# Attention: scores and turned queries and keys ahead of the transposed probabilities, within a slot's group of short matmuls

## The chip, the cores and the metric

The kernel runs on one core of one Trainium2 chip. The metric is the device time of one execution in microseconds (us); lower is better. TensorE (PE in the profile, with its weight loads as PEld), VectorE (DVE), ScalarE (ACT), GpSimd (POOL) and the DMA queue of SyncE (SP) each work through a list of their own and wait for each other by semaphores.

## The reference

A decoder trunk of two layers over one sequence of 1024 tokens of width 1024, in float32. The first layer's mixer has two parts that share one input projection: a gated spatial mixing of 128-token chunks, and an attention of eight heads of width 64. Only the attention bears on the change:

```
B_BRANCHES = ((128, 1), (512, 4), (2048, 16))       # window, dilation
qh, kh = rms_norm(heads(q), q_g), rms_norm(heads(k), k_g)
for window, dilation in B_BRANCHES:
    # keys of the own and the previous block of 128, of every dilation-th token
    s = where(valid, q @ k.T * hd ** -0.5, NEG)
    m = max(s); p = exp(s - m); den = sum(p)
    o = (p @ v) / den;  lse = m + log(den)
b_out = sum over branches of softmax(lse) * o
```

After it come the output projection, a gated MLP with a causal convolution, and a second layer with gated linear attention and the same kind of MLP.

## The kernel before

The attention works by pairs of heads, four pairs in all. A pair has 16 units: eight near units (kind "n", dilation 1, one for each block of 128 queries) and eight far units (kind "d", tokens by stride 4, with the third branch folded in by a mask). `order` lists them as near 0 to 7 and far 0 to 7 of pair 0, then of pair 1, and so on: 64 units, each with a slot of its own. I count slots from 0; slots 16 to 23, for instance, are the near units of the second pair.

A unit has three steps on TensorE. `score` multiplies queries by keys (two fp32r matmuls, the high and the low part of the keys, for each of the two heads) into the PSUM tile `sc`. VectorE adds the mask and takes the row minimum of the negated scores (L895), and ScalarE makes the exponentials in `sm` and their sum (L896). `turn` transposes `sm` on TensorE into the PSUM tile `pP` (L916), which is copied to `pT`: by VectorE for even units, by ScalarE for odd ones (L918). `output` multiplies `pT` by the values into `po` (L927). The three steps of one unit stand in three slots that follow each other: the scores in its own, the transposes in the next, the output in the one after.

For near units the queries and keys of a block are first turned themselves: `Pair.turn` transposes the duplicated keys `kd` (L997) and the split queries `qs` (L122) into the PSUM tile `tk`, of which there is one buffer. ScalarE and VectorE split it into `kT` (L116, L117), and ScalarE copies the queries to `qT` (L1002). This is done two slots ahead of the unit, so 30 of the 64 slots hold such turns.

Between these short matmuls TensorE works at the projection of the next pair (`pj`, later `pv` and `pu`, L218): `take(share)` issues 13, 12 or 21 of its matmuls in each slot. Meanwhile ScalarE and VectorE make the next weights `wq`, `wv` from raw ones (L767, L768), normalise queries and keys (L964 to L973), and combine the near and far results of the pair before (`combine`, L1037 to L1056, in the slots of near units 4 and 6).

TensorE's order is the order in which the code issues (`pin` keeps it). The order on the other engines is set by a scheduler that works out when each instruction would be ready, so it can move when TensorE's order is changed. Buffers: `sm` 3, `pT` 2, and in PSUM `sc` 2, `pP` 2, `pj` 2, `po` 1, `tk` 1.

Of the kernel before, what the change touches and what calls it, by code (L numbers as in the profile page):

```python
# [67 lines left out]
def trunk(ctx: ExitStack, tc: tile.TileContext, a, out):  # L68
# [581 lines left out]
    def even(gm_open):  # L650
        with ExitStack() as st:
# [69 lines left out]
            with tc.tile_pool(name="at", bufs=2, reuse_waits="tile") as at, \  # L721
                    tc.tile_pool(name="av", bufs=1, reuse_waits="tile") as av:
                return attention(ps, at, av, pq, pq0, par0, wx, wq0, gqk, masks, rest, gm_open)
# [152 lines left out]
    def attention(ps, at, av, pq, pq0, par0, wx, wq0, gqk, masks, rest, gm_open):  # L876
# [59 lines left out]
        class Pair:  # L936
# [46 lines left out]
            def parts(self, n):  # L983
                qn = self.qn[n]
                qs = pq.tile([P, 2, P], F32R, tag="qs", bufs=2, name=f"qs{self.p}{n}")
                split([qs[:, :, :64], qs[:, :, 64:]], heads(qn[:, :P]), hi=G.tensor_copy)
                kd = pq.tile([P, 2, P], F32, tag="ks", bufs=2, name=f"kd{self.p}{n}")
                G.tensor_tensor(kd.rearrange("p h (x c) -> p h x c", x=2),
                                heads(qn[:, P:])[:, :, None, :].to_broadcast([P, 2, 2, 64]),
                                gqk[:, None, None, :].to_broadcast([P, 2, 2, 64]), op=ALU.mult)  # L990
                self.qs[n] = qs, kd
# [39 lines left out]
        def combine(q, g):  # L1031

            p, os = q.p, [q.near[g]["ot"], q.on[g]]
            nm = [o[:, :, 128:130] for o in os]
            den = [o[:, :, 130:132] for o in os]
            M = small.tile([P, 4, 2], F32, tag="cM", bufs=2, name=f"cM{p}{g}")
            tc.keep_in_program_order(V.tensor_tensor(M, nm[0], nm[1], op=ALU.min))  # L1037
            e = small.tile([P, 2, 4, 2], F32, tag="cE", bufs=2, name=f"cE{p}{g}")
            for i in range(2):
                V.tensor_sub(e[:, i], M, nm[i])  # L1040
            A.activation(e, e, AF.Exp)
            return lambda: combined(p, g, os, den, e)
# [22 lines left out]
        def weights():  # L1065
            if slot and spread:
                spread.pop(0)()
# [4 lines left out]
        def mix(when):  # L1072
            while mixes and when(mixes[0]):
                mixes.pop(0)[2]()
# [16 lines left out]
        def take(m):  # L1091
            for _ in range(m):
                ins = next(stream, None)
                if ins is not None:
                    if pairs[0].done > 1:
                        tc.keep_in_program_order(ins)
# [16 lines left out]
        def turns(i):  # L1113
            p, kind, n = place_of(i)
            if kind == "n":
                pairs[p].turn(n)
# [9 lines left out]
        ended, scored = [], []  # L1126
        for slot, (p, kind, n) in enumerate(order):
            share = RATE[0] if slot < NT else RATE[1] if len(pairs) < PAIRS or pairs[-1].done < NT else RATE[2]
            parts(slot + 3)
            score, turn, output = pairs[p].near_unit(n) if kind == "n" else pairs[p].far_unit(n)  # L1130
            for f in ended:
                f()
            for f, _ in scored:
                f()
            score()
            turns(slot + 2)
            mix(lambda m: m[0] <= slot)
            weights()
            take(share // 2)
            weights()  # L1140
            take(share - share // 2)
            ended, scored = [f for _, f in scored], [(turn, output)]
            if kind == "n" and p and n in (4, 6):
                combine(pairs[p - 1], n // 2 - 2)()
# [588 lines left out]
```

## Time and profile before

| | us |
|---|---|
| median of 3 runs | 2114.88 |
| lowest, highest | 2114.22, 2115.79 |
| the profiled execution's own time | 2114.53 |
| its span, first to last instruction | 2112.8 |
| TensorE busy | 2102.1 |
| VectorE busy | 1533.2 |
| ScalarE busy | 1058.7 |

The attention's slots lie between about 34 and 318 us of the span. In the profile a row of the timeline has the start, the time from there to the end of the last one merged into it, engine, line, operation, the tiles written and read, their shape and the count. Starts of weight loads (PEld) show the pace of TensorE better than the ends of matmuls, which are modelled. A row of the waits has the engine and tile that waited, the releaser, and the total, the count and the longest. Tile names in the trace lack their last numbers: `sm1n` is any `sm` of the near units of pair 1. A wait of TensorE lengthens the run directly; a wait of another engine does only if TensorE has to wait for it in turn.

### The profile page before, as it was taken

Reading aid. Unit: us, or ns where it says so; the run is one execution under the profiler, and the core shown is the slowest. Engines: PE = TensorE matmul, PEld = TensorE weight load, DVE = VectorE, ACT = ScalarE, POOL = GpSimd, SP = SyncE. Lnnn points to the kernel's source line nnn. Section 1 sums busy time; section 2 is a strip of 40 time slices with the busy share of each in tenths; the row PEclk is TensorE's granted clock in tenths of the full one; section 3 lists DMA queues with packets and bytes.
Section 4 is the critical chain, followed back from the end, with each engine's and each line's share of the span. In section 5 each row is a group of like instructions: output and inputs, shape, how many; then the busy total and the mean of one; then the engine's idle time right before and its main releaser. Section 6 shows DMA issues by size and latency. Waiting matters only on the chain. (4 is left out here: it accounts for less than half of the span.)

```text
span 2112.8 us, 29740 instructions
## 1 busy us (share of the span) xinstructions
PE 2102.1 (99%) x10440; PEld 1793.6 (85%) x10440; DVE 1533.2 (73%) x2486; ACT 1058.7 (50%) x2063; POOL 471.3 (22%) x479
## 2 busy tenths in 40 slices
PE   8999999999999999999999999999999999999999
PEld 8999988888888888888899888888888888888887
DVE  7566564678889888655578777886788788785554
ACT  7566564455444444444454466745544444444443
POOL 5344310014335243000010011101334243220000
PEclk9999999999999999999999999999999999999999
DMA  7122314854544444765654243596544454458564
GB/s 256 53 75 65 106 46 173 306 197 145 177 142 159 160 163 168 259 220 205 216 182 158 88 137 125 182 325 240 193 163 151 167 164 158 152 181 294 208 227 162
DMA packets 170278, 367.08 MB, mean 174 GB/s; under 512 B 17632, under 2 KB 61408, under 8 KB 170128
## 3 DMA queue, kind: packets, MB, share of 16 engines
q1 hardware_dynamic: 169984, 365.05, 50.5%
q8 instruction: 82, 1.34, 0.3%
q14 instruction: 68, 0.56, 0.1%
q10 hardware_dynamic: 144, 0.13, 0.0%
HBM read 248.39 MB, written 115.93 MB: 172 GB/s over the span
## 5 line engine op out<-in xcount | busy, mean ns | idle before, releaser
L117 DVE TENSOR_TENSOR da<-ar,da 128x512 fp32r<-128x512 f32 x154 | 106.2, 690 | 154.7 <-ACT da L116 154.5
L116 ACT CAST da<-ar 128x512 fp32r<-128x512 f32 x154 | 96.0, 623 | 212.7 <-PE pdQ L427 99.5
L218 PE MATMUL po<-wo,hq 128*128 128x512 f32 x768 | 183.0, 394 | 0.0
L218 PEld LDWEIGHTS po<-wo,hq 128*128 128x128 f32 x768 | 142.0, 188 | 28.5 <-DVE hq L117 0.3
L218 PE MATMUL pv<-wv,hq 128*128 128x512 f32 (+2 forms) x768 | 139.7, 339 | 0.0
L427 PE MATMUL pdC<-dw,da 128*128 128x512 f32 x528 | 134.8, 390 | 0.0
L427 PE MATMUL pdB<-dw,da 128*128 128x512 f32 x528 | 134.8, 390 | 0.0
L218 PEld LDWEIGHTS pv<-wv,hq 128*128 128x128 f32 x768 | 119.4, 189 | 14.7
L218 PE MATMUL pj<-wq,hq 128*128 128x384 f32 x672 | 128.6, 339 | 0.0
L427 PEld LDWEIGHTS pdC<-dw,da 128*128 128x128 f32 x528 | 99.0, 188 | 20.5
L427 PEld LDWEIGHTS pdB<-dw,da 128*128 128x128 f32 x528 | 98.8, 188 | 20.3
L218 PEld LDWEIGHTS pj<-wq,hq 128*128 128x128 f32 x672 | 114.8, 188 | 0.0
L286 POOL TENSOR_TENSOR S1g<-rg 128x512 f32<-128x512 f32 x20 | 28.5, 1427 | 378.6 <-DMA wsd<-D 262.2
L117 DVE TENSOR_TENSOR dw<-wr,dw 128x512 fp32r<-128x512 f32 x154 | 105.7, 686 | 8.4 <-ACT dw L116 8.0
L161 POOL TENSOR_SCALAR rn<-ssq 128x1 f32<-128x1 f32 x22 | 8.8, 402 | 424.9 <-ACT h L181 242.4
L427 PE MATMUL pdO<-dw,da 128*128 128x512 f32 x396 | 100.5, 389 | 0.0
L116 ACT CAST dw<-wr 128x512 fp32r<-128x512 f32 x154 | 95.0, 617 | 8.6 <-DMA wr<-in_w_dn 4.9
L427 PEld LDWEIGHTS pdO<-dw,da 128*128 128x128 f32 x396 | 74.3, 188 | 15.4
L351 DVE SCALAR_TENSOR_TENSOR t<-g,cw,t 128x1022 f32<-128x1022 f32 x44 | 74.8, 1700 | 0.1
L335 DVE TENSOR_TENSOR g<-g,s1g 128x512 f32<-128x512 f32 x22 | 16.4, 745 | 77.8 <-ACT s1g L334 77.8
L350 DVE SCALAR_TENSOR_TENSOR t<-g,cw,t 128x1023 f32<-128x1023 f32 x44 | 57.3, 1302 | 14.8 <-ACT t L349 14.8
L161 POOL TENSOR_SCALAR ro<-oss 128x1 f32<-128x1 f32 x32 | 9.4, 292 | 255.6 <-ACT og L1448 255.6
(1052 smaller groups left out, 5440.6 us busy)
## 6 DMA issues: line engine op xcount, KB each, us to landing
ar<-actd SPq DMA_DIRECT2D x70, 512.0 KB, 3.6
rd<-in_w_down SPq DMA_DIRECT2D x44, 512.0 KB, 3.6
wsd<-D SPq DMA_DIRECT2D x88, 256.0 KB, 2.3
rg<-in_w_gate SPq DMA_DIRECT2D x40, 512.0 KB, 3.6
ru<-in_w_up SPq DMA_DIRECT2D x40, 512.0 KB, 4.5
wr<-wsd SPq DMA_DIRECT2D x40, 512.0 KB, 4.3
actd<-t SPq DMA_DIRECT2D x66, 256.0 KB, 2.2
wr<-in_w_dn SPq DMA_DIRECT2D x30, 512.0 KB, 5.0
```

The lines of the kernel that those rows point to most:

```text
L116: (hi or A.copy)(dst[0], src)
L117: (lo or V.tensor_sub)(dst[1], src, f32(dst[0]))
L161: eng.tensor_scalar(r, ssq, 1.0 / n, EPS, op0=ALU.mult, op1=ALU.add)
L218: yield T.matmul(o, L[i], R[jj][:, sl], start=(k == 0 and (ii, jj) == PASSES[0]), stop=(k == nk - 1 and (ii, jj) == PASSES[-1]))
L286: G.tensor_tensor(sums[name], x, y, op=op)
L335: V.tensor_add(C22, C22, s1)
L350: V.scalar_tensor_tensor(t[:, 1:], g[:, : S - 1], w(1), t[:, 1:], op0=ALU.mult, op1=ALU.add)
L351: V.scalar_tensor_tensor(t[:, 2:], g[:, : S - 2], w(0), t[:, 2:], op0=ALU.mult, op1=ALU.add)
L427: T.matmul(o, L[ii][:, t * P : t * P + P], R[jj], skip_group_check=more, start=start and not more and (ii, jj) == PASSES[0], stop=stop and ...
```

## The change

In each slot the two lines that run `turn` of the unit before (`scored`) move behind the scores, the turned queries and keys, and the mixing. The outputs (`ended`) stay ahead.

```diff
             for f in ended:
                 f()
-            for f, _ in scored:
-                f()
             score()
             turns(slot + 2)
             mix(lambda m: m[0] <= slot)
+            for f, _ in scored:
+                f()
             weights()
             take(share // 2)
```

TensorE in slot 21 (near unit 5 of pair 1), before; `pP1n4` are the transposed probabilities of unit 4, `sc1n5` the scores of unit 5, `tk17` the turned keys and queries of block 7:

```order
L916 MATMUL pP1n4_1871<-ident_78,sm1n40_1819 128x128 x2
L916 MATMUL pP1n4_1871<-ident_78,sm1n41_1825 128x128 x2
L890 MATMUL sc1n50_1878<-kT1_965,qT15_1765 128x256 x2
L890 MATMUL sc1n51_1884<-kT1_965,qT15_1765 128x256 x2
L997 MATMUL tk17_1890<-ident_78,kd17_1802 128x128 x2
L122 MATMUL tk17_1890<-identr_83,qs17_1799 128x128 x2
```

The same place of the changed kernel:

```order
L890 MATMUL sc1n50_1871<-kT1_965,qT15_1758 128x256 x2
L890 MATMUL sc1n51_1877<-kT1_965,qT15_1758 128x256 x2
L997 MATMUL tk17_1883<-ident_78,kd17_1802 128x128 x2
L122 MATMUL tk17_1883<-identr_83,qs17_1799 128x128 x2
L916 MATMUL pP1n4_1893<-ident_78,sm1n40_1812 128x128 x2
L916 MATMUL pP1n4_1893<-ident_78,sm1n41_1818 128x128 x2
```

The four transposes of unit 4 have moved from the head of the group to its end.

VectorE in slot 21, before; `on00` is the weighted far part of the pair before, `pT1n4` the copy of `pP1n4`:

```order
L1054 TENSOR_TENSOR on00_1626<-on00_1626,cE00_1852 128x4x128
L918 COPY pT1n4_1876<-pP1n4_1871 128x512
L895 ISA sm1n50_1881,ot1n4_1815<-sc1n50_1878,mband_308 128x4x64
L895 ISA ot1n4_1815 128x1
L895 ISA sm1n51_1887,ot1n4_1815<-sc1n51_1884,mband_308 128x4x64
L895 ISA ot1n4_1815 128x1
L1056 TENSOR_TENSOR ot0n0_743<-ot0n0_743,on00_1626 128x4x128
L117 TENSOR_TENSOR kT1_965<-tk17_1890,kT1_965 128x8x32
```

And in the changed kernel:

```order
L1054 TENSOR_TENSOR on00_1626<-on00_1626,cE00_1852 128x4x128
L895 ISA sm1n50_1874,ot1n4_1808<-sc1n50_1871,mband_308 128x4x64
L895 ISA ot1n4_1808 128x1
L895 ISA sm1n51_1880,ot1n4_1808<-sc1n51_1877,mband_308 128x4x64
L895 ISA ot1n4_1808 128x1
L1056 TENSOR_TENSOR ot0n0_743<-ot0n0_743,on00_1626 128x4x128
L117 TENSOR_TENSOR kT1_965<-tk17_1883,kT1_965 128x8x32
L918 COPY pT1n4_1898<-pP1n4_1893 128x512
```

The copy has moved from the front of the scores' two reductions to the place behind the sum and the split of `kT`. In the other slots with a copy on VectorE it moves behind the two reductions in the same way.

ScalarE between slots 17 and 18, before; `qT13` is the copy of the turned queries of block 3, `wq24` to `wq26` are pieces of the next weights:

```order
L966 ACTIVATE vN16_1662<-pj16_1555,r0_89 128x128
L1002 CAST qT13_1654<-tk13_1647 128x256
L767 ACTIVATE wq24_1438<-wq22r_1331,g0_88 128x384
L767 ACTIVATE wq25_1484<-wq22r_1331,g0_88 128x384
L767 ACTIVATE wq26_1493<-wq23r_1333,g0_88 128x384
```

And in the changed kernel:

```order
L966 ACTIVATE vN16_1662<-pj16_1555,r0_89 128x128
L767 ACTIVATE wq24_1438<-wq22r_1331,g0_88 128x384
L1002 CAST qT13_1649<-tk13_1642 128x256
L767 ACTIVATE wq25_1484<-wq22r_1331,g0_88 128x384
L767 ACTIVATE wq26_1493<-wq23r_1333,g0_88 128x384
```

One piece of the weights now stands ahead of the copy of the queries.

## The prediction

> **What bounds the kernel now.** I read the page's busy shares first, then the waits of the weight loads, then the stretches of the attention stage, and only then single slots.
>
> ```profile
> PE 2102.1 (99%) x10440; PEld 1793.6 (85%) x10440; DVE 1533.2 (73%) x2486; ACT 1058.7 (50%) x2063; POOL 471.3 (22%) x479
> 97.20:130.20 33.00, 33.00 (x248) 33.00 (x248) 24.78 (x79) 20.79 (x64) 17.78 (x27) 1.00 0.29 83
> ```
>
> The second row is a stretch of eight slots (the near units of the second pair): length, then busy time of PE, PEld, DVE, ACT, POOL, and the granted clock, 1.00. TensorE has no idle time there, VectorE 8.2 us (33.00 - 24.78), about 1.0 us a slot. So a slot costs what TensorE's sequence costs, and the change can do three things: remove waits of TensorE, make new ones, or change how fast the same short matmuls follow each other. First the waits in the attention stage which the change can reach:
>
> ```profile
> PEld pP0n L916 <- ACT sm0n L896: 1.0, 2, 0.6
> PEld pP2d L916 <- ACT sm2d L896: 0.3, 1, 0.3
> PEld pP0d L916 <- ACT sm0d L896: 0.2, 1, 0.2
> PEld pP1d L916 <- ACT sm1d L896: 0.2, 1, 0.2
> ```
>
> Five times in 64 slots TensorE waits for an exponential before it turns the probabilities: 1.7 us in total. This is all that can be won from waits.
>
> **Waits that go: -1.7, and +0.3 back.** The transposes of the probabilities (pP) now stand behind the scores (sc) and, in 30 of the 64 slots, behind the turned keys and queries (tk). In the rows of a slot with all four groups (starts of the weight loads) that is 0.44 us later for the scores and 0.41 for the turns:
>
> ```profile
> 117.62 0.30 PEld L927 LDWEIGHTS po1n<-vN,pT1n 128*128 128x128 f32 x2
> 117.79 0.48 PEld L916 LDWEIGHTS pP1n<-ident,sm1n 128*128 128x128 f32 x4
> 118.23 0.54 PEld L890 LDWEIGHTS sc1n<-kT,qT 128*128 128x128 f32 x4
> 118.72 0.24 PEld L997 LDWEIGHTS tk<-ident,kd 128*128 128x128 f32 x2
> 118.93 0.25 PEld L122 LDWEIGHTS tk<-identr,qs 128*128 128x128 f32 x2
> 119.13 0.30 PEld L218 LDWEIGHTS pj<-wq,hq 128*128 128x128 f32 x2
> ...
> 121.17 0.59 PEld L927 LDWEIGHTS po1n<-vN,pT1n 128*128 128x128 f32 x4
> ```
>
> The largest wait (0.6) falls in a slot with turns, which gives 0.9 us. The three waits of 0.2 to 0.3 fall in far slots without turns, where the scores alone give about 0.45. So all five are covered. One comes back in another place, in the second slot:
>
> ```profile
> 38.25 0.14 PEld L916 LDWEIGHTS pP0n<-ident,sm0n 128*128 128x128 f32 x1 [0.36 <-ACT sm0n L896]
> 38.80 0.24 PEld L997 LDWEIGHTS tk<-ident,kd 128*128 128x128 f32 x2
> ```
>
> On ScalarE at that time:
>
> ```profile
> 38.10 0.35 ACT L1002 CAST qT<-tk 128x256 fp32r<-128x256 f32 x1
> ```
>
> The turns there need the one PSUM buffer that this copy of qT empties at 38.45. Without the wait of 0.36 and without pP ahead, they would come at about 38.25 and wait 0.2 to 0.3. I take +0.3.
>
> **Pace of the short matmuls: +1.2.** The number of matmuls is unchanged; what can differ is the step at the joins between the groups. Removed are the joins po to pP, pP to sc, and tk (or sc) to the projection; added are po to sc, tk (or sc) to pP, and pP to the projection. The trace has one case or a neighbour of each. From po to an fp32r product, at the stage's end:
>
> ```profile
> 320.75 0.30 PEld L927 LDWEIGHTS po3d<-v,pT3d 128*128 128x128 f32 x2
> 320.97 0.30 PEld L218 LDWEIGHTS pu<-wu,hq 128*128 128x128 f32 x2
> ```
>
> From fp32r transposes (identr) to fp32 ones (ident) and back, in the output projection:
>
> ```profile
> 356.00 0.25 PEld L122 LDWEIGHTS pc<-identr,cat 128*128 128x128 f32 x2
> 356.20 0.20 PEld L122 LDWEIGHTS pc<-ident,mx 128*128 128x128 f32 x2
> 356.37 0.25 PEld L122 LDWEIGHTS pc<-identr,cat 128*128 128x128 f32 x2
> ```
>
> And a slot without turns:
>
> ```profile
> 183.64 0.48 PEld L916 LDWEIGHTS pP2n<-ident,sm2n 128*128 128x128 f32 x4
> 184.09 0.54 PEld L890 LDWEIGHTS sc2n<-kT,qT 128*128 128x128 f32 x4
> 184.56 0.31 PEld L218 LDWEIGHTS pj<-wq,hq 128*128 128x128 f32 x2
> ```
>
> From po to pP the two loads took 0.17 (117.62 to 117.79), from po to an fp32r product 0.22 (320.75 to 320.97): the new join po to sc costs 0.05 more. Around the fp32r transposes the steps are 0.20 and 0.17 for two each (356.00, 356.20, 356.37), the neighbour of tk to pP.
>
> A slot with turns: before, from the first pP to the projection, 0.44 + 0.49 + 0.21 + 0.20 = 1.34. Now 0.05 + sc 0.49 + tk 0.21 + 0.20 + pP (0.17 for the first two, 0.22 for the last two) = 1.34. Nothing changes.
>
> A slot without turns: before 0.92 (183.64 to 184.56). Now 0.05 + sc 0.49 (with the step to an fp32 transpose, as 118.23 to 118.72) + pP 0.21 (first two as tk at 118.72) + 0.22 = 0.97. That is +0.05. There are 34 such slots; 22 have scores 256 wide as in these rows (1.1 us), for the 12 with narrow scores I take 0.01. Together +1.2. The bounds, by the spread of these steps, are -0.04 in each of the 64 slots (-2.6) and +0.07 (+4.5). By the Trainium skill ("TensorE: Matmul & The Clock Gate", section "LDWEIGHTS (loading the stationary operand)") a load's time goes by its columns alone, about 107 ns for 128, so order would cost nothing and the whole sum would be 1.2 lower; the trace agrees within a group (0.44 for four) and not at the join after po.
>
> **The copy behind the scores' reductions: +1.4.** Each pP is copied from PSUM to pT, for even units on VectorE, and pT feeds po at the head of the next slot. By the order of the changed kernel this copy now stands behind both reductions of the scores (L895) of its slot, and in the slot of unit 5 of a pair also behind the sum L1056 and the split of kT:
>
> ```profile
> 118.54 0.69 DVE L1054 TENSOR_TENSOR on<-on,cE 128x512 f32<-128x512 f32 x1
> 119.15 0.68 DVE L918 COPY pT1n<-pP1n 128x512 f32<-128x512 f32 x1
> 119.75 0.63 DVE L895 CUSTOM_DVE_ANT_1 sm1n<-sc1n,mband 128x256 f32<-128x256 f32 x1
> ...
> 120.28 0.62 DVE L895 CUSTOM_DVE_ANT_1 sm1n<-sc1n,mband 128x256 f32<-128x256 f32 x1
> ...
> 120.80 0.69 DVE L1056 TENSOR_TENSOR ot0n<-ot0n,on 128x512 f32<-128x512 f32 x1
> 121.40 0.42 DVE L117 TENSOR_TENSOR kT<-tk,kT 128x256 fp32r<-128x256 f32 x1
> ```
>
> The same place in the third pair:
>
> ```profile
> 180.71 0.68 DVE L918 COPY pT2n<-pP2n 128x512 f32<-128x512 f32 x1
> ```
>
> VectorE runs without a gap here. With the copy last, the reductions start at 119.15 and 119.68, the sum at 120.20, the split at 120.80, the copy at 121.13 and ends at 121.81; po wants it at 121.17 (row above). TensorE waits 0.64 and some 0.05 for the signal, 0.7. The third pair has the same sequence (the copy at 180.71, again right behind the product with the weights of the combining), so twice 0.7. In the first pair the combining does not happen, and in the last one the slots are stretched by wider matmuls. The ends: 0, if VectorE comes to this point 0.7 earlier because nothing holds it in the slot before; 3, if the combining is 0.8 later than now. The Trainium skill says (same page, "Architectural detail: the array is 16× 32×32, not 1× 128×128") that ScalarE's and VectorE's queues are strictly first in, first out; by it the copy cannot overtake, which these rows agree with.
>
> **Later qT: +0.4.** In three slots (18, 34, 50) ScalarE now makes one piece of the next weights before the copy of qT:
>
> ```profile
> 104.65 0.37 ACT L1002 CAST qT<-tk 128x256 fp32r<-128x256 f32 x1
> 104.90 1.14 ACT L767 ACTIVATE wq<-wq22r,g 128x384 fp32r<-128x384 f32 x2
> 105.92 0.61 ACT L767 ACTIVATE wq<-wq23r,g 128x384 fp32r<-128x384 f32 x1
> ```
>
> The turns on TensorE in the slot after:
>
> ```profile
> 105.92 0.24 PEld L997 LDWEIGHTS tk<-ident,kd 128*128 128x128 f32 x2
> ```
>
> One piece is 0.51 (half of 104.90 to 105.92), so qT ends at 105.53 instead of 105.02. The turns, which come 0.44 earlier, want the buffer at 105.48: a wait of 0.1, and 0.2 where the weights are 512 wide. The ends are 0 and 1.5 (0.5 each). Other queues: GpSimd's order shifts by single places, SP's three times by one DMA; neither is on TensorE's path by more than the qT case, and I cost them at nothing.
>
> **Sum.** -1.7 + 0.3 + 1.2 + 1.4 + 0.4 = +1.6 on the profiled execution's 2114.53, which lies 0.35 below the median of the runs. Against the median: 2116.5.
>
> **The rivals.** First, a wait in every slot. The sm pool has three buffers, two for each unit, so the second reduction of a slot writes the buffer that pP's first pair reads. Before, pP stood ahead of the scores; now VectorE must wait for it, and behind the waiting reduction stand the copy of pT, the split of kT and pieces of the next weights.
>
> ```profile
> L916 PE MATMUL pP1n<-ident,sm1n x30: 272/273/282, 101.5 to 130.2; 128*128 128x128 f32 x30
> ```
>
> After the scores come 0.21 + 0.20 of turns, 0.22 of pP and 0.27 until its result; the first reduction covers 0.53: VectorE waits up to 0.37 in a slot with turns. It decides only where VectorE's idle 1.0 us a slot is used up; if it reached TensorE in full, 30 x 0.37 = 11 us (2127.6); half of that gives 2122. For it: VectorE has runs without gaps, as above. Against it: other work stands between the two reductions in some slots. Chance 0.11.
>
> Second, VectorE catches up: the scores start 0.44 earlier in each group, no new wait appears and the pace stays: 2114.9 - 1.7 = 2113.2. Against it: the gapless rows of the copy. Chance 0.12.
>
> Third, the joins go the good way in all slots (-2.6) besides the removed waits: 2110.6, faster. Against it: the row at 320.97. Chance 0.03.
>
> **How the numbers follow.** The case of the sum has 0.74 and a range of its own from 2114.3 to 2119.4 (new waits of none to 3, pace of 0 to 3). A measurement of this kernel can tell about 0.2%, 4.2 us. Slower by that is the first rival and the sum's own tail (0.03): 0.14. Faster is the third rival: 0.03. The rest, 0.83, is the same. The range that leaves out no more than 2 in 10 goes from the second rival to the near part of the first: 2113.2 to 2120.2.
>
> **What would show it.** The waits of pP for exponentials should be gone from the list; po should wait for the copy of pT in the two slots after unit 5 of the second and third pair, 0.5 to 1 us each; tk should wait for qT about four times, 0.1 to 0.3. Slots without turns should be 0.05 longer, slots with turns unchanged. VectorE's second reduction should show idle time ended by pP. I am wrong if po waits in most slots with turns, or if the pace changes by 0.1 or more a slot.

## The result, and the profile after

| | before | after |
|---|---|---|
| median of the runs compared, us | 2115.34 (22 runs) | 2118.61 (22 runs) |
| lowest, highest | 2114.08, 2116.92 | 2117.59, 2120.11 |
| the profiled execution's own time | 2114.53 | 2118.09 |
| its span | 2112.8 | 2116.4 |
| granted clock | 1.00 | 1.00 |

The ratio is 1.0016, with a 95% interval from 1.0010 to 1.0022: the changed kernel is 3.3 us slower, less than the 0.2% that I took as the bound of what can be told, and yet outside the noise of 22 runs each. The forecast was 2116.5, with a range from 2113.2 to 2120.2.

The busy shares of the page after hardly differ from those before; they could not have told the direction:

```profile
PE 2104.0 (99%) x10440; PEld 1794.6 (85%) x10440; DVE 1541.7 (73%) x2486; ACT 1054.0 (50%) x2063; POOL 468.7 (22%) x479
```

The waits of TensorE's weight loads in the attention stage of the changed kernel (who waited, the releaser; total, count, longest):

```profile
PEld tk L997 <- issue: 1.4, 4, 0.5
PEld tk L997 <- POOL rq L161: 1.0, 1, 1.0
PEld po1n L927 <- ACT qT L1002: 0.9, 1, 0.9
PEld po2n L927 <- ACT qT L1002: 0.9, 1, 0.9
PEld tk L997 <- POOL kd L988: 0.2, 1, 0.2
...
```

All five waits of pP for an exponential are gone. In their place stand five waits of the turns (tk; 0.2 and four with "issue", of up to 0.5) and two of po, 0.9 each. The tk wait of 1.0 is in the start-up, at 31.5 us. For po the view names ScalarE's copy of qT; the rows below show that it was the copy of pT on VectorE.

For the account I took the start of the first po matmul of each slot from both traces; the difference of two neighbours is what that slot gained or lost:

| where | us |
|---|---|
| up to the first po (start-up, slot 1) | +0.16 |
| slots 2 to 5 | -0.05 |
| slots 12, 28 and 44, where pP waited (-0.12, -0.12, -0.26) | -0.50 |
| slots 19, 35 and 51: tk waits (+0.25, +0.29, +0.47) | +1.00 |
| slots 21 and 37, to the po at the head of the next: po waits (+0.77, +0.75) | +1.52 |
| the other 51 intervals: pace | +1.77 |
| up to the po of the last slot | +3.89 |

The span ends 3.6 us later. The start-up term differs from trace to trace: over the eleven kernels other than the one before, with one trace each, it lay between -0.16 and +0.49. I read nothing into it.

### The profile page after: what moved, and what is told of

The parts are those of the page before. It is cut to its first block, busy times and chain, and to the rows that moved or that the text cites. A ratio compares the mean times of both kernels' runs of the same rounds, so it can differ in the third digit from the quotient of the medians.

```text
span 2116.4 us, 29735 instructions
## 1 busy us (share of the span) xinstructions
PE 2104.0 (99%) x10440; PEld 1794.6 (85%) x10440; DVE 1541.7 (73%) x2486; ACT 1054.0 (50%) x2063; POOL 468.7 (22%) x479
```

## The pace, as the rows show it

A slot without turns in the changed kernel, weight loads:

```profile
186.13 0.42 PEld L927 LDWEIGHTS po2n<-vN,pT2n 128*128 128x128 f32 x3
186.46 0.54 PEld L890 LDWEIGHTS sc2n<-kT,qT 128*128 128x128 f32 x4
186.95 0.47 PEld L916 LDWEIGHTS pP2n<-ident,sm2n 128*128 128x128 f32 x4
187.39 0.48 PEld L218 LDWEIGHTS pj<-wq,hq 128*128 128x128 f32 x3
```

The last three po loads to the scores take 0.33, three even steps of 0.11. Before, the last step, from po to pP, was 0.06: four po loads from 183.25 to 183.64 took 0.39, where four even steps of 0.11 would be 0.45. The row of the kernel before:

```profile
183.25 0.53 PEld L927 LDWEIGHTS po2n<-vN,pT2n 128*128 128x128 f32 x4
```

From the first of the two short groups to the projection it is 0.93 now (186.46 to 187.39), 0.92 before (183.64 to 184.56): the loss is the join behind po. Slots with turns lose the same join, but win another. Their transposes now stand behind the turned queries, and from the first transpose to the second it is 0.06 instead of 0.12 (slot 20). The four with their join took 0.44 before (117.79 to 118.23, in the prediction) and take 0.39 now (119.33 to 119.72, below). Summed over the slots without any wait, the 21 with wide scores lost 1.29 (0.06 each), the 10 with narrow ones 0.29 (0.03 each), the 19 with turns 0.19 (0.01 each).

## Which slots lose: two runs that split the change

The first run moves the transposes only in the 34 slots without turns, the second only in the 30 with turns:

```diff
+            late = place_of(slot + 2)[1] != "n"     # first run; == "n" in the second
             for f, _ in scored:
-                f()
+                if not late:
+                    f()
             score()
             turns(slot + 2)
             mix(lambda m: m[0] <= slot)
+            for f, _ in scored:
+                if late:
+                    f()
```

> The move is made only in the 34 slots without turned queries and keys. My theory (the loss is a sum: 0.05 us of pace in each slot without turns, 1.5 for the copy of pT behind the combining, 1.0 for qT that comes late, less 0.7 for three waits that go): +1.6 - 0.5 to -0.7, so +1.0 us against the kernel before; no wait of po for the copy, no wait of tk for qT in slots 19, 35 and 51. Rival (the ring of three sm buffers delays VectorE, and all waits follow from that): the ring costs nothing in slots without turns, so +0 or below.

> The move is made only in the 30 slots with turned queries and keys. My theory: the copy's wait 1.5, the late qT 1.0, pace 0.2, first slots 0 to 0.2, so +2.7 us against the kernel before, with the three waits of 0.2 to 0.3 in slots 12, 28 and 44 still there; with the run before this gives the whole change. If the parts hang together rather than add up, the two halves do not add to the whole's 3.3.

Measured against a median of 2114.88 for the kernel before (33 runs on the same chip; here and below the kernel in question has 11 runs, and the interval of its ratio is about 1.9 us to each side, so the slots of the traces decide on parts of a microsecond): 2115.52 and 2117.51, ratios 1.0003 (0.9994 to 1.0012) and 1.0011 (1.0002 to 1.0020). The losses, 0.64 and 2.63, add up to the 3.3 of the whole change. In the trace of the first run slots 12, 28 and 44 gain 0.50, one new wait of 0.2 stands before a po (in slot 40), and the other slots without turns cost 1.60 with it. In the second the tk waits cost 0.96 and the po waits 1.56. At the last po the two traces stand at +0.91 and +2.94, against +3.89 for the whole. So the slots without turns lose by pace more than they win by waits, and the slots with turns carry the larger part of the loss.

## The order of the two transposes

Is it the distance from the head of the slot, or that the transposes stand behind the turns? This run puts them between the scores and the turns, in all slots:

```diff
             for f in ended:
                 f()
+            score()
             for f, _ in scored:
                 f()
-            score()
             turns(slot + 2)
```

> The transposes of the probabilities stand between the scores and the turned queries and keys in every slot. By the joins in the rows (from po to sc, from sc to pP, from pP to tk and from tk to the projection) now slots with turns lose 0.05 too: pace +1.6 + 1.5 = +3.1. The turns come as late as before, so tk does not wait for qT in slots 19, 35 and 51; the copy of unit 4 comes 0.4 earlier and stands ahead of the combining's sum, so po waits 0 to 0.3 each; the five waits of pP go (-1.7). In all +1.4 to +2.0 against the kernel before. Rival (pace does not depend on the order): -1.7 to -1.0.

2116.84, ratio 1.0009 (1.0000 to 1.0018), 1.96 above its kernel before. Waits of its weight loads:

```profile
PEld tk L997 <- issue: 0.5, 1, 0.5
PEld po1n L927 <- DVE pT1n L918: 0.4, 1, 0.4
PEld po2n L927 <- DVE pT2n L918: 0.4, 1, 0.4
...
```

The transposes come 0.41 earlier than in the changed kernel, and po no longer waits in slots 22 and 38. The two waits of 0.4 are those of the next copy on VectorE (unit 6) and stand at the head of slots 24 and 40; here the view names the copy of pT. The tk waits of slots 19, 35 and 51 all but vanish, 0.21 instead of 1.00. In return the 19 slots with turns that have no wait cost 1.03 instead of 0.19, 0.05 each. They had the slow join behind po in the changed kernel too; what they lose here is the short step behind the turned queries, which is 0.11 again (slots 18 and 20). So the pace depends on what stands behind what, and the waits on how early the turns and how late the copy come.

## The late qT: not the piece of the weights, but VectorE's split

Slot 19 of the changed kernel, in the timeline of the weight loads:

```profile
109.65 0.54 PEld L890 LDWEIGHTS sc1n<-kT,qT 128*128 128x128 f32 x4
110.42 0.20 PEld L997 LDWEIGHTS tk<-ident,kd 128*128 128x128 f32 x2 [0.23 <-issue]
```

ScalarE of the same kernel, up to the copy of qT for which these turns wait:

```profile
108.66 0.51 ACT L896 ACTIVATE sm1n<-sm1n,ot1n 128x256 f32<-128x256 f32 x1
109.07 0.19 ACT L896 ACTIVATION_READ_ACCUMULATOR sm1n<-sm1n,ot1n 128x1 f32 x1
109.98 0.37 ACT L1002 CAST qT<-tk 128x256 fp32r<-128x256 f32 x1 [0.72 <-DVE kT L117]
```

And its VectorE from slot 18 on:

```profile
106.12 0.69 DVE L895 CUSTOM_DVE_ANT_1 sm1n<-sc1n,mband 128x256 f32<-128x256 f32 x1
...
106.66 0.97 DVE L768 SCALAR_TENSOR_TENSOR wq<-wq22r,g,wq 128x384 fp32r<-128x384 f32 x1
107.55 0.47 DVE L973 SCALAR_TENSOR_TENSOR qn<-pj,r,rq 128x256 f32<-128x256 f32 x1
107.95 0.61 DVE L895 CUSTOM_DVE_ANT_1 sm1n<-sc1n,mband 128x256 f32<-128x256 f32 x1
...
108.47 1.09 DVE L768 SCALAR_TENSOR_TENSOR wq<-wq23r,g,wq 128x384 fp32r<-128x384 f32 x1
109.48 0.41 DVE L117 TENSOR_TENSOR kT<-tk,kT 128x256 fp32r<-128x256 f32 x1
```

The turns wait for the copy of qT, which empties the tk buffer at 110.35. ScalarE was free from 109.26 on and sat idle 0.72: it waited for VectorE's split of kT, which ends at 109.89. In all 32 blocks of both kernels the copy of qT begins after that split has ended, by 0.03 us at the least, though it needs nothing of it: both read the PSUM tile tk. The Trainium skill ("PSUM — Partial Sum Buffer", section "PSUM bank collisions raise a hardware error ⚠️") says that accesses of two engines to one bank must be kept apart, two reads by ScalarE and VectorE too, and that the compiler's scheduler adds a dependency for it; these rows agree with the order, though no run here shows a collision.

VectorE of the kernel before, in the same slot:

```profile
106.29 0.61 DVE L895 CUSTOM_DVE_ANT_1 sm1n<-sc1n,mband 128x256 f32<-128x256 f32 x1
...
106.82 0.62 DVE L895 CUSTOM_DVE_ANT_1 sm1n<-sc1n,mband 128x256 f32<-128x256 f32 x1
...
107.34 0.62 DVE L768 SCALAR_TENSOR_TENSOR wq<-wq22r,g,wq 128x384 fp32r<-128x384 f32 x1
107.87 0.61 DVE L768 SCALAR_TENSOR_TENSOR wq<-wq23r,g,wq 128x384 fp32r<-128x384 f32 x1
108.40 0.48 DVE L973 SCALAR_TENSOR_TENSOR qn<-pj,r,rq 128x256 f32<-128x256 f32 x1
108.80 0.41 DVE L117 TENSOR_TENSOR kT<-tk,kT 128x256 fp32r<-128x256 f32 x1
```

The second reduction (107.95 in the changed kernel) now stands behind a piece of the weights and qn; before, it stood right behind the first. But the same five operations stand ahead of the split in both, without a gap: two reductions, two pieces and qn. From the start of the first reduction to the split it is 3.36 now (106.12 to 109.48) and was 2.51 (106.29 to 108.80). This 0.85 lies in the two pieces, which take 0.97 and 1.09 now and took 0.62 and 0.61: in their new places they run beside operations of GpSimd (last section). In slots 34 and 50 it is the same: 3.37 against 2.51 and 3.42 against 2.77.

The next run gives `sm` a fourth buffer in the changed kernel, so that the second reduction need not wait for the transposes that read the third:

```diff
-            sm = at.tile([P, 256], F32, tag="sm", name="sm" + name, bufs=3)[:, :W]
+            sm = at.tile([P, 256], F32, tag="sm", name="sm" + name, bufs=4)[:, :W]
```

> The changed kernel with four sm buffers in place of three, so that no reduction of the scores has to wait for the transposes of the unit before. My theory: VectorE's idle time between the two reductions of a slot goes, but the waits of po (1.5) and tk (1.0) stay, since they hang on what stands ahead of the copy and of qT in the queues: the same as the changed kernel within 0.3 us. Rival (the ring): the waits of tk and po go, 2.0 to 2.5 us below the changed kernel.

2116.78, ratio 1.0008 (1.0000 to 1.0017), 1.9 above its kernel before and so 1.4 better than the changed kernel. Its VectorE in the same slot:

```profile
106.13 0.64 DVE L895 CUSTOM_DVE_ANT_1 sm1n<-sc1n,mband 128x256 f32<-128x256 f32 x1
...
106.67 0.62 DVE L895 CUSTOM_DVE_ANT_1 sm1n<-sc1n,mband 128x256 f32<-128x256 f32 x1
...
108.66 0.42 DVE L117 TENSOR_TENSOR kT<-tk,kT 128x256 fp32r<-128x256 f32 x1
```

And the waits of its weight loads in the attention stage:

```profile
PEld tk L997 <- POOL rq L161: 1.0, 1, 1.0
PEld po2n L927 <- ACT qT L1002: 0.8, 1, 0.8
PEld po1n L927 <- ACT qT L1002: 0.8, 1, 0.8
PEld tk L997 <- issue: 0.2, 1, 0.2
```

The reduction stands where it stood before the change, both pieces take 0.61, the split ends 0.81 earlier (109.08 instead of 109.89), and the waits of tk in slots 19, 35 and 51 are gone (+0.03 in the three instead of +1.00). So my theory of the late qT fell, and the ring of three sm buffers that I had as a rival has a part in it, though not in the form that I gave the rival. VectorE does not stand and wait for pP in every slot; its scheduler puts other work ahead of the reduction. In slots 18, 34 and 50 two pieces of the weights then meet GpSimd and take longer, and that makes the split, qT and the turns of the next slot late.

Two later runs show that it is this meeting, and not the place of the reduction. With qT first in the changed kernel (below), the reduction of slot 18 stands behind a piece too, but no piece takes longer, and the split begins 2.53 after the first reduction. With qT first in the kernel before, the two reductions stand side by side, but one piece takes 1.02, and it is 2.92.

Slot 4 is another matter. It is 0.40 shorter with the fourth buffer and 0.07 without, but that only takes back a start that was 0.33 later: in both, ScalarE makes qT at 51.53, behind its work on the next block, and the turns begin at 51.96 and 51.97. The po waits, too, stay at 0.8.

## The copy of pT

Slot 21 of the changed kernel on VectorE:

```profile
119.87 0.62 DVE L895 CUSTOM_DVE_ANT_1 sm1n<-sc1n,mband 128x256 f32<-128x256 f32 x1
...
120.39 0.62 DVE L895 CUSTOM_DVE_ANT_1 sm1n<-sc1n,mband 128x256 f32<-128x256 f32 x1
...
120.93 0.69 DVE L1056 TENSOR_TENSOR ot0n<-ot0n,on 128x512 f32<-128x512 f32 x1
121.53 0.42 DVE L117 TENSOR_TENSOR kT<-tk,kT 128x256 fp32r<-128x256 f32 x1
121.87 0.69 DVE L918 COPY pT1n<-pP1n 128x512 f32<-128x512 f32 x1
```

Its weight loads up to po at the head of slot 22:

```profile
119.33 0.42 PEld L916 LDWEIGHTS pP1n<-ident,sm1n 128*128 128x128 f32 x4
119.72 2.04 PEld L218 LDWEIGHTS pj<-wq,hq 128*128 128x128 f32 x12
122.67 0.97 PEld L927 LDWEIGHTS po1n<-vN,pT1n 128*128 128x128 f32 x8 [0.91 <-ACT qT L1002]
```

The transposes were in PSUM by about 120; the copy began at 121.87, behind both reductions, the sum and the split, and ended at 122.56. po follows 0.11 later. To test that it is this copy, the changed kernel with the copy of unit 4 of the second and third pair on ScalarE:

```diff
-                (A.copy if i % 2 else V.tensor_copy)(pT[:, :, :nj, :], pts)
+                (A.copy if i % 2 or name in ("1n4", "2n4") else V.tensor_copy)(pT[:, :, :nj, :], pts)
```

> The changed kernel with one edit: the copy of unit 4's transposed probabilities (near units of the second and third pair) is made by ScalarE instead of VectorE. Theory (the waits of po in slots 22 and 38, 0.9 us a gap and 1.5 us in the slots' lengths, come from that copy's place behind VectorE's reductions, sum and split): both waits go, 1.3 to 1.6 us less than the changed kernel, about 2117.0; the waits of tk in slots 19, 35 and 51 stay (1.0). If instead po waits because something else in slots 21 and 37 is late (the values or the one po buffer), nothing changes: within 0.4 us of the changed kernel.

2116.90, ratio 1.0010 (1.0002 to 1.0019), 1.74 above its kernel before (2115.16): 1.5 better. Of its waits in this stage the row that bears on it:

```profile
PEld tk L997 <- issue: 2.3, 6, 0.8
...
```

po is not in the list any more; slots 21 and 37 are 0.02 shorter than before the change. The waits of tk in slots 19, 35 and 51 stay, 0.94. Both causes taken out together, with the fourth sm buffer and the copy on ScalarE:

> The changed kernel with two edits: four sm buffers instead of three, and the copy of unit 4 on ScalarE as in the run beside it. Theory (the loss is three separate things that add: tk waits 1.0 to 1.4 by the ring of three sm buffers, po waits 1.5 by the copy, pace 1.8): tk waits and po waits are both gone, 2.5 to 3.0 us less than the changed kernel, and what stays against the kernel before is the pace of 0.05 in each slot without turns less the removed waits of pP, 0 to +0.8. If the two waits share one cause, or one hides behind the other, the saving is that of one alone, 1.4 to 1.6.

2115.50, ratio 1.0002 (0.9993 to 1.0011), 0.34 above its kernel before. Each alone took off 1.4 and 1.5, together 2.9 of the 3.3; in the traces, from slot 6 on, 1.2, 1.8 and 2.8. The two are separate and add. In its trace only the pace is left (1.51), less the gain in slots 2 to 5 (0.39) and in slots 12, 28 and 44 (0.50), and 0.25 in the start-up.

## Another way to an early qT

Here the changed kernel issues the copy of qT ahead of the split of kT, so that ScalarE no longer waits for VectorE:

```diff
-                split([four(self.kT[:, i * 2 : i * 2 + 2], n) for i in range(2)], by4(t[:, :2]))
                 qT = pq.tile([P, 2, P], F32R, tag="qT", bufs=3, name=f"qT{self.p}{n}")
                 A.copy(qT, t[:, 2:])
+                split([four(self.kT[:, i * 2 : i * 2 + 2], n) for i in range(2)], by4(t[:, :2]))
```

> The changed kernel with one edit: the copy of the turned queries qT is issued ahead of the split of kT. Theory (the late qT in slots 4, 19, 35 and 51 is a matter of what stands ahead of it on ScalarE and VectorE, above all the split of kT behind the delayed second reduction): those waits of tk go, 1.0 to 1.4 us less than the changed kernel, and the waits of po in slots 22 and 38 stay (1.5 us). Rival (tk's buffer is released late by the split of kT on VectorE itself, whatever the order): the releaser in the list of waits changes from qT to kT, and the time stays within 0.4 us of the changed kernel.

2115.14 against 2115.16, ratio 1.0002 (0.9992 to 1.0011): by the times the whole loss is gone, 3.3 us, more than I expected, because the po waits go too. In the trace +0.59 is left at the last po: the pace (1.53) stays, against gains of 0.55 in slot 4 and 0.50 in slots 12, 28 and 44. VectorE in slot 21:

```profile
118.90 0.63 DVE L895 CUSTOM_DVE_ANT_1 sm1n<-sc1n,mband 128x256 f32<-128x256 f32 x1
...
119.44 0.62 DVE L895 CUSTOM_DVE_ANT_1 sm1n<-sc1n,mband 128x256 f32<-128x256 f32 x1
...
119.97 0.68 DVE L918 COPY pT1n<-pP1n 128x512 f32<-128x512 f32 x1
120.57 0.68 DVE L1056 TENSOR_TENSOR ot0n<-ot0n,on 128x512 f32<-128x512 f32 x1
121.17 0.42 DVE L117 TENSOR_TENSOR kT<-tk,kT 128x256 fp32r<-128x256 f32 x1
```

The copy now stands ahead of the sum and the split and ends at 120.65, and po begins without a wait at 120.99. Behind the two reductions alone it is early enough; it is the sum and the split (0.94, from 120.93 to 121.87) that made it late. This run thus does not tell the two causes apart (it mends both). Why the copy moved up I take to be that the scheduler now counts the split as ready later; no run shows it.

## A version that beats both?

Two tries to keep only what the move wins. First, the kernel before with a fourth sm buffer, and with the move in slots 4, 12, 28 and 44 alone:

```diff
+            late = slot in (4, 12, 28, 44)
             for f, _ in scored:
-                f()
+                if not late:
+                    f()
...
+            for f, _ in scored:
+                if late:
+                    f()
```

> The kernel before with two edits: only in slots 4, 12, 28 and 44 (four of the five in which pP waited for an exponential; in the fifth, slot 1, the move only trades it for a wait of tk) do the transposed probabilities stand behind scores and turns, and sm has four buffers. Theory (what can be won are the waits, the pace costs 0.05 only in moved slots without turns): 0.12 + 0.12 + 0.26 less 0.15 counted in, and about 0.35 in slot 4, so 0.7 to 1.0 us less than the kernel before. Rival (what a slot gains is given back downstream, since VectorE and ScalarE set the long-run pace): within 0.2 us of the kernel before.

2114.57 against 2115.16, ratio 0.9997 (0.9988 to 1.0005). Slots 12, 28 and 44 are shorter by 0.15, 0.15 and 0.29, and nothing gives it back up to the last slot (-0.66 there). Slot 4 gains nothing (+0.01): its turns wait instead, as its row of the weight loads shows.

```profile
51.78 0.20 PEld L997 LDWEIGHTS tk<-ident,kd 128*128 128x128 f32 x2 [0.58 <-POOL rq L161]
```

Second, the move in slots 1, 4, 12, 28 and 44 with the copy of qT first, and beside it the kernel before with the copy of qT first alone:

> The kernel before with two edits: the copy of qT ahead of the split of kT, and only in slots 1, 4, 12, 28 and 44 (the five in which pP waited) the transposed probabilities behind scores and turns. Theory (the waits are won, the pace costs nothing where slots are left alone, the turns of slot 4 no longer wait for a late qT): 0.15 + 0.15 + 0.29 in the three far slots and 0.4 to 0.55 in slot 4, so 1.0 to 1.2 us less than the kernel before, about 2114.0; slot 1 gives nothing (its wait turns into one of tk). Rival (the new place of qT costs in the other slots with turns, since kT comes 0.25 later): less than 0.5 us gained.

> The kernel before with the copy of qT ahead of the split of kT alone, the order of the short matmuls unchanged. Theory (the earlier qT repairs what the changed order did to the turns and to the copy of pT, and has nothing to repair here): within 0.4 us of the kernel before, the five waits of pP still in the list. Rival (qT first is a gain of its own, which the run with both would owe to it): 1 us or more less than the kernel before.

2114.14 and 2115.42 against 2115.37, ratios 0.9994 (0.9985 to 1.0003) and 1.0000 (0.9991 to 1.0009). In the traces slot 4 gains 0.55 in both: that gain belongs to the earlier qT, and not, as I had expected, to the move. With qT first ScalarE made the exponential that pP waited for at 50.14 instead of 50.95, ahead of the work on the next block (ScalarE of the second of the two):

```profile
50.14 0.49 ACT L896 ACTIVATE sm0n<-sm0n,ot0n 128x256 f32<-128x256 f32 x1
...
50.63 0.45 ACT L964 ACTIVATE qn<-pj,r 128x256 f32<-128x256 f32 x1
```

Part of it is lost again in slot 2 (+0.25 and +0.32), where pP has a new wait for an exponential, 0.29 and 0.37. In the second of the two the waits of slots 1 and 4 are thus gone, and of the five that I expected to stay only the three far ones did. The move itself gives 0.58 in the three far slots, and nothing that can be seen in slot 1. At the last slot the two stand at -0.94 and -0.26. These are gains that the traces show slot by slot; by the times alone no version is shown to be faster than the kernel before.

## Why the prediction came out

Its terms, against the account above:

- **Waits that go, -1.7, and +0.3 back.** The five waits went. The three far ones gave what they were (-0.50 with 0.15 of pace inside). Of the two early ones, 0.36 in slot 1 came back as a tk wait of 0.23, as said, and 0.59 in slot 4 came back as one of 0.47, which I had not seen. The term was about -0.9 in place of -1.4. The failed step: "The largest wait (0.6) falls in a slot with turns, which gives 0.9 us". That covers the exponential, but the turns themselves then come 0.4 and the missing wait earlier and stand before a tk buffer that is no more ready than it was. I had checked this in slot 1 only.
- **Pace, +1.2.** 0.06 and 0.03 for the slots without turns, 0.01 with turns, in place of 0.05, 0.01 and 0: about 1.9 with the 0.15 in the three far slots. The mechanism is the join behind po, 0.11 instead of 0.06, and in slots with turns the short step behind the turned queries that gives it back, as said; the size was short by 0.7. The rule on load times of the Trainium skill that I had weighed ("TensorE: Matmul & The Clock Gate", section "LDWEIGHTS (loading the stationary operand)"), by my estimate from it about 107 ns for each, fits the new join and not the old one, which was shorter; by it the term would have been 0.
- **The copy of pT, +1.4.** +1.52, in the two slots named, by the mechanism named, which the copy on ScalarE confirmed. I had 0.05 for the signal; po began 0.11 after the copy's end.
- **Later qT, +0.4.** +1.00. Right kind of wait, wrong cause and one slot later. The piece of the weights ahead of qT did no harm in slots 18, 34 and 50. I looked only at what stands ahead of qT in ScalarE's list, not at what it waits for: the split on VectorE. The step that failed is "GpSimd's order shifts by single places", costed at nothing. GpSimd's cast of slot 18 had moved one place (105.29 before, 106.55 now) and a piece on VectorE to the same moment; this meeting and a second one made the split 0.85 late.
- **The sum** of +1.6 was 1.7 to 2 short: 0.5 from slot 4 and slot 1, 0.7 from the pace, 0.6 from qT. All were on the same side; the pace, the copy and qT each lay inside the bounds given for them, and the time inside the range of the sum. The direction hung on the copy: without its +1.4 the sum would have been +0.2.
- **The rivals.** The first (the ring of three sm buffers) was right about the resource and wrong about the price: three slots, not thirty, and 1.0 us in their lengths. In the stretch of the eight near slots of the second pair VectorE's reductions sat idle for pP 0.6 us in total, in two of them; in the whole stage the view lists 22 such waits, 6.3 us. The second (VectorE catches up) and the third did not happen.

## What to carry to other kernels

When short work is moved in front of other short work on the bounding engine, look at the moved-up group too: it now asks earlier for its own buffer, and that buffer's release runs over every reader, on all engines, in their order. A copy that feeds the next slot is priced by what stands ahead of it in its engine's list after the change, not by its length. And the lengths in the old profile hold beside the old neighbours: here the same piece of work took up to 0.48 longer at its new place. Where a scheduler sets those lists, one operation written two lines earlier (here the copy of qT) undid the whole loss of the change.

## What the runs showed of the hardware

The same piece of the next weights on VectorE took 0.61 us in most places, and 0.97 and 1.09 in slot 18 of the changed kernel (rows above). GpSimd had begun shortly before each of the two:

```profile
106.55 0.66 POOL L1003 CAST qR<-qT 128x256 fp32r<-128x256 f32 x1
...
108.41 0.73 POOL L988 TENSOR_TENSOR kd<-qn,gqk 128x256 f32<-128x256 f32 x1
```

With qT first, VectorE began such a piece 0.21 ahead of the same cast, at 106.41, and took 0.61; the cast took longer:

```profile
106.62 0.93 POOL L1003 CAST qR<-qT 128x256 fp32r<-128x256 f32 x1 [0.27 <-ACT qT L1001]
```

In these rows whoever began second was stretched, by 0.27 to 0.48. There are 288 such pieces in the traces of the twelve kernels. The 197 that ran beside neither this cast nor this product took 0.60 to 0.64. Those begun 0.05 to 0.13 behind one of the two took 0.94 to 1.10, those begun 0.26 to 0.28 behind 0.80 or 0.81. Those begun ahead took 0.60 to 0.65, and GpSimd's operation took longer instead (the cast up to 0.97, the product up to 1.08). The Trainium skill ("SBUF — State Buffer", section "Who interferes with whom") says that an operation of VectorE with two inputs from SBUF contends with a GpSimd operation that reads SBUF, and that the order of issue decides who is held up; the rows agree. Of the 0.85 by which the split of slot 18 is late, the two pieces make 0.83. No run took this away and left all else: the fourth sm buffer moved the order with it.
